# Moving stores to GpSimd's queue, fetching the first SwiGLU weights during w_out, interleaving two standard pairs by column group, and other pages for mid tiles

## The chip, the cores and the metric

The kernel runs on one core of a Trainium2 chip. The metric is the device time of one execution in microseconds (us). The kernel before took 1378.4 us, the median of three runs (1376.95 to 1379.79).

## The reference

One layer of a hybrid decoder on 1056 tokens (a prompt of 1024, and 8 sequences of 4 tokens with states of their own), D_MODEL 1024, all in float32. What matters here is the second half of the layer:

```python
merged = sigmoid(g_ssm) * br_ssm + sigmoid(g_pool) * br_pool
x  = x + gate1 * (merged @ w_out)                      # 1024 x 1024
h2 = rmsnorm(x, norm2_g) * (1 + scale2) + shift2
f_a, f_b = split(h2 @ w_ffn_in, 2)                     # 1024 x 2 * 2816
x  = x + gate2 * ((silu(f_a) * f_b) @ w_ffn_out)       # 2816 x 1024
y  = rmsnorm(x, normf_g)
```

Before it stand the modulation by the conditioning, the first norm, the input projection, a diagonal state-space mixer and a pooling mixer.

## The kernel before

All activations lie with features on the 128 partitions and the 1056 tokens along the free dimension, in eight tiles of 128 features. A product is made of three matmuls in a rounded format: each operand is split into a hi part (a cast) and a lo part (the rest), and hi x hi, hi x lo and lo x hi are summed (`feat`, L508). `split` (L487) makes the two parts of a weight tile: a cast on ScalarE (L491) and a subtraction on VectorE (L492). `load` (L482) fetches 512 KB of weights on SP into one of two `raw` buffers. The tokens are cut into three column groups, `GROUPS`: 0 to 384, 384 to 768, 768 to 1056.

The order of the instructions on TensorE and on SP's queue is that of the program. The order on VectorE, ScalarE and GpSimd is set by the build, by a schedule on a simulated time line. Work that is to run beside the matmuls is put among them by a `Pump` (L433): a generator that yields estimated microseconds; after each step of `feat` it is told how many have passed (`tick`, 3 x columns / 2400 a step), and it goes on when its time is due.

**w_out** (L1016 to L1031). Eight output tiles d for each column group g. w_out's first tile comes from the `wts` pool, the other seven lie split in the pool pE. After each product `residual` (L970) adds it to X[d], and `square` (L549) adds the squares to acc. In the last column group the finished X[d] is stored to DRAM (xr, L1028) on SP. After each column group its `norm2` is pumped: `rstd` (L578) sums acc over the partitions (L585), takes the reciprocal root on VectorE and spreads it by matmuls (L592) into R (L594); then for each of the eight tiles GpSimd multiplies x by R (L1002), ScalarE makes the hi part of h2 (L1003), VectorE the whole of it (`full`, L1008) and the lo part (L1012), and SP stores `full` to DRAM (hd, L1013). `full` has two buffers in pE for the first two groups; for the third it lies in acc's columns.

**ffn_in, standard pairs** (L1048, called at L1142). The hidden tiles k = 0 and 1 (NS = 2) of 22 are done in the ordinary way, one after the other, each with its three column groups: two products of eight steps (a and b), silu of a (L1059), times b (L1060), then `put_mid` (L1040) splits the result into mh and ml (L1043, L1044) and stores both to DRAM (md, L1046) on GpSimd's queue. The weights come through `ahead` (L499), which fetches and splits one tile ahead of the one in use. norm2 of the third group is still pumped during k = 0 and drained before its third group; `sums` follows on the pump.

**sums** (L1068). The pairs from k = 2 on use seven products in place of eight for a 2 x 2 block of features and tokens. `sums` builds the sums of h2's quarters that they need: for each of four tiles it fetches four quarters (bq, L1072) from hd on SP, makes four sums on VectorE (L1075 to L1078), and splits them into th and tl (L1085, L1086). bq, the sums and the tiles of put_mid share one ring of nine buffers in pool pF (`quart`, L1036). X's pages and acc's are reused by th and tl.

**Fast pairs** (L1154, called at L1196). `prep` (L1104) makes the seven weight operands of a pair, each with its hi part (L1109) and lo part (L1110), and `product` (L1127, matmuls L1133 to L1135) multiplies them. `ring` (L1098) says where each operand lies: three in pF with three buffers, four in `wts` with four. The operands of k = 2 are loaded and made after the standard pairs in the program.

**w_ffn_out** (L1216 to L1278). Three blocks of six hidden tiles, each for eight d, then a last stage of four hidden tiles (18 to 21) with the final norm. `fetch_mid` (L1208) brings mh and ml of one hidden tile back from DRAM on GpSimd's queue, into pages of the pool pP (26 pages, shared with X) or into the six buffers of `gpage` in pool pG (L1227). The tiles of the next block are asked for after d = 1 of each block (L1250).

Of the kernel before, what the change touches and what calls it, by code (L numbers as in the profile page):

```python
# [11 lines left out]
F32R = mybir.dt.float32r  # L12
# [443 lines left out]
def trunk(ctx: ExitStack, tc: tile.TileContext, A, O):  # L456
    nc = tc.nc
# [41 lines left out]
    def ahead(srcs):  # L499

        nxt = split2(srcs[0])
        for i in range(len(srcs)):
            cur, nxt = nxt, split2(srcs[i + 1]) if i + 1 < len(srcs) else None
            yield cur
# [3 lines left out]
    def feat(ps, w, x, g, kts, first=True, last=True):  # L508

        a, b = cols(g)  # L510
        for kt in kts:
            (wh, wl), (xh, xl) = w(kt), x(kt)
            pe.matmul(ps, wh, xh[:, a:b], start=first and kt == kts[0], stop=False)  # L513
            pe.matmul(ps, wh, xl[:, a:b], start=False, stop=False)  # L514
            pe.matmul(ps, wl, xh[:, a:b], start=False, stop=last and kt == kts[-1])  # L515
            tick(3 * (b - a) / 2400)

    def mmg(g):
        a, b = cols(g)
        return mm((128, b - a))  # L520
# [76 lines left out]
    def modulate_samples(xs, am, sm, k, t):  # L597

        bc = lambda m: m[:, k, None, 1:9].to_broadcast([128, 4, 8])
        f = lambda z: z.rearrange("p (s b) -> p s b", b=8)  # L600
        v.tensor_mul(f(t), f(xs), bc(am))
        v.tensor_add(f(t), f(t), bc(sm))
# [389 lines left out]
    def norm2(g):  # L992
        a, b = GROUPS[g]
        e = min(b, ST)
        yield 3.0
        for us in rstd(acc, g, R, 5.0):
            yield us if isinstance(us, float) else 1.0
        for k in range(8):
            t, (hi, lo) = tmp("xn"), h2x(k)
            sc, sh = mod[4][:, k, 0:1], mod[3][:, k, 0:1]  # L1000
            n = e - a
            gp.tensor_mul(t[:, 0:b - a], X[k][:, a:b], R[:, a:b])  # L1002
            act.activation(hi[:, a:e], t[:, 0:n], AF.Identity, bias=sh, scale=sc)  # L1003
            if g < 2:
                full = pE.tile([128, 384], F32, name="full", tag="full", bufs=2)
            else:
                full = acc[:, GROUPS[(g - k) % (g + 1)][0]:][:, 0:b - a]
            v.tensor_scalar(full[:, 0:n], t[:, 0:n], sc, sh, op0=MUL, op1=ADD)  # L1008
            if b > ST:
                modulate_samples(t[:, n:n + 32], mod[4], mod[3], k, full[:, n:])  # L1010
                act.copy(hi[:, e:b], full[:, n:])
            v.tensor_sub(lo[:, a:b], full[:, 0:b - a], fp(hi[:, a:b]))  # L1012
            nc.sync.dma_start(hd[k, :, a:b], full[:, 0:b - a])  # L1013
            yield 1.0

    with pool("pE") as pE:  # L1016
        wo = [next(wgen)]
        for d in range(1, 8):
            raw = load(A["w_out"][d])
            wo.append([split(raw[:, i], pE, "wo", 14) for i in range(2)])  # L1020
        for g in range(3):
            for d in range(8):
                ps = mmg(g)
                feat(ps, w8(wo[d]), mx, g, range(8))
                residual(d, g, ps, mod[2])
                square(X[d], g, acc, d == 0)
                if g == 2:
                    nc.sync.dma_start(xr[d], X[d])  # L1028
            pumps.append(Pump(norm2(g)))
        while len(pumps) > 1:  # L1030
            pumps.pop(0).drain()  # L1031
# [2 lines left out]
    third = ExitStack()  # L1034
    pF = third.enter_context(pool("pF"))
    quart = lambda n, dt=F32: pF.tile([128, 528], dt, name=n, tag="Q", bufs=9)  # L1036
    NS = 2
    wgen = ahead([A[n][k] for k in range(NS) for n in ("w_ffn_a", "w_ffn_b")])

    def put_mid(m, k, cut, eng=None):  # L1040

# [3 lines left out]
        for i, z in enumerate((hi, lo)):  # L1045
            gp.dma_start(md[k][:, i, cut], z)  # L1046

    def ffn_in(k, wa, wb):  # L1048
        for g in range(3):
            a, b = GROUPS[g]  # L1050
            n = b - a
            pa, pb = mmg(g), mmg(g)
            if k == 0 and g == 2:
                pumps.pop(0).drain()
                pumps.append(Pump(sums()))
            feat(pa, w8(wa), h2x, g, range(8))
            feat(pb, w8(wb), h2x, g, range(8))
            t = tmp("sa")
            act.activation(t[:, 0:n], pa, AF.Silu)  # L1059
            v.tensor_mul(t[:, 0:n], t[:, 0:n], pb)  # L1060
            put_mid(t[:, 0:n], k, slice(a, b))

# [3 lines left out]
    def sums():  # L1068
        for k in range(4):
            q = [quart("bq") for _ in range(4)]  # L1070
            for i, z in enumerate(q):
                nc.sync.dma_start(z, hd[k + 4 * (i // 2), :, 528 * (i % 2):528 * (i % 2) + 528])  # L1072
            b11, b12, b21, b22 = q
            f = {j: quart("bf") for j in (5, 3, 4, 6)}
            v.tensor_sub(f[4], b12, b22)  # L1075
            v.tensor_sub(f[5], f[4], b11)
            v.tensor_sub(f[3], b11, b12)
            v.tensor_add(f[6], f[5], b21)  # L1078
            for js in ((5, 3), (4, 6)):
                new = (lambda n: page(n, F32R)) if js[0] == 5 or k < 1 else (  # L1080
                    lambda n: pF.tile([128, NTOK], F32R, name=n, tag="T", bufs=6))
                hi, lo = new("th"), new("tl")
                for i, j in enumerate(js):
                    h, l = (z[:, 528 * i:528 * i + 528] for z in (hi, lo))
                    act.copy(h, f[j])  # L1085
                    v.tensor_sub(l, f[j], fp(h))  # L1086
                    TB[k, j] = (h, l)
            yield 6.0
# [8 lines left out]

    def ring(n, i):  # L1098
        t = "whi" if n == "whi" else "wlo"
        if i in (0, 3, 5):  # L1100
            return pF.tile([128, 512], F32R, name=n, tag="r" + t, bufs=3)
        return wts.tile([128, 512], F32R, name=n, tag=t, bufs=4)

    def prep(a11, a12, a21, a22):  # L1104
# [34 lines left out]
        ra, rb = load(A["w_ffn_a"][k]), load(A["w_ffn_b"][k])  # L1139
        return prep(ra[:, 0], ra[:, 1], rb[:, 0], rb[:, 1])  # L1140

    for k in range(NS):  # L1142
        wa = next(wgen)
        ffn_in(k, wa, next(wgen))
    for p in pumps:
        p.drain()
    pumps.clear()
# [87 lines left out]
    for bi, ks in enumerate(blocks):  # L1235
        for d in range(8):
            w, i = nxt, 8 * bi + d + 1
            nxt = o6(i) if i < 24 else None
            if bi == 2 and d >= 4:
                o4(d - 4)  # L1240
            pss = [mmg(g) for g in G3]
            for j, k in enumerate(ks):
                wd = lambda kt: tuple(z[:, 128 * (j % 3):128 * (j % 3) + 128] for z in w[j // 3])
                for g in range(3):
                    feat(pss[g], wd, lambda kt: mids[k], G3[g], [0], j == 0, j == 5)
            for g in range(3):
                residual(d, G3[g], pss[g], mod[5])
            if d == 1:
                for k in ((6, 7, 8, 9, 10, 11), (12, 13, 14, 15, 16, 17), (18, 19, 20, 21))[bi]:
                    fetch_mid(k, gpage if k in (9, 10, 11, 15, 16, 17, 20, 21) else mpage)  # L1250

    LAST = ((0, CUT[0]), CUT, (CUT[1], NTOK))
    acc3, R3 = page("acc3"), page("R3")
# [98 lines left out]
```

## Time and profile before

| | before |
|---|---|
| median of three runs | 1378.4 us (1376.95 to 1379.79) |
| the profiled execution | 1382.86 us, its span 1380.4 us |
| TensorE busy | 1318.2 us, 95% of the span |
| VectorE busy | 791.7 us, 57% |
| ScalarE busy | 440.3 us, 32% |
| GpSimd busy | 192.6 us, 14% |
| granted clock of TensorE, mean | 0.973 of 2.4 GHz |

The profile is of one execution; its times count from the span's start. Engines are named PE (TensorE, matmuls), PEld (its weight loads, which overlap the matmuls), DVE (VectorE), ACT (ScalarE), POOL (GpSimd) and SP; SPq and POOLq are the queues on which SP and GpSimd issue transfers. L1013 is line 1013 of the kernel. A matmul's duration runs to its modelled end and overlaps the next one, so the pace is read from starts.

### The profile page before, as it was taken

To read this page: it belongs to the slowest core of one execution; us is meant where nothing else is said; L and a number is where in the kernel's file an instruction comes from. 1 tells how busy PE (TensorE), PEld (TensorE's weight loads), DVE (VectorE), ACT (ScalarE), POOL (GpSimd) and SP (SyncE) were. 2 spreads that over 40 slices of the span, in tenths; PEclk is the share of its full clock that TensorE was granted. 3 is DMA by queue.
4 is the path that set the end of the run, shared out by engine and by line. 5 is a ranking of instruction groups with operands and counts; after the bars stand their busy time and mean duration, and the time that the engine had idled before them with its cause. 6 is when DMAs were issued, how large, how long until landed. Compare 5 with 4: busy or idle time off the path is not lost.

```text
span 1380.4 us, 23211 instructions
## 1 busy us (share of the span) xinstructions
PE 1318.2 (95%) x9248; PEld 1260.9 (91%) x9248; DVE 791.7 (57%) x1765; ACT 440.3 (32%) x840; POOL 192.6 (14%) x315
## 2 busy tenths in 40 slices
PE   5889999999999999979899999999999999999996
PEld 2789899999988899978899999999999999999985
DVE  8876895942115555665866666666666433333346
ACT  5423342234622332223433333333333211111124
POOL 3211222021000000222101001101101321000004
PEclk8899999999999999998999999999999999999998
DMA  9242213043535532153533333323323895232303
GB/s 382 85 132 62 77 52 91 23 113 118 180 128 170 185 131 77 47 202 119 166 108 109 105 98 109 110 93 109 121 82 109 308 350 174 75 116 78 94 24 126
DMA packets 75259, 173.95 MB, mean 126 GB/s; under 512 B 9808, under 2 KB 29456, under 8 KB 75152
## 3 DMA queue, kind: packets, MB, share of 16 engines
q1 hardware_dynamic: 47424, 105.77, 23.2%
q0 software_dynamic: 25280, 63.86, 14.1%
q10 hardware_dynamic: 2448, 2.84, 0.6%
q8 instruction: 72, 1.18, 0.4%
q14 instruction: 35, 0.29, 0.1%
HBM read 130.17 MB, written 42.27 MB: 125 GB/s over the span
## 4 chain that ended last, share of the span: by engine, by line
PE 38%; issue 10%; DVE 2%; DMA 2%; POOL 0%; DVEq 0%; ACT 0%; SPq 0%; POOLq 0%; ACTq 0%
PE b L1135 10%; PE b L1133 10%; PE b L1134 10%; PE mm L514 3%; PE mm L515 3%; PE mm L513 3%; DMA bq<-hd 1%; DMA ml<-md 1%; DMA mh<-md 0%; DVE tl L1086 0%; PE aux L592 0%; DVE xf L1264 0%; DVE bf L1075 0%; POOL mh L1211 0%; DVE sa L1060 0%
## 5 line engine op out<-in xcount | busy, mean ns | idle before, releaser
L513 PE MATMUL mm<-hh,whi 128*128 128x384 f32 (+1 forms) x864 | 290.4, 336 | 15.3 <-ACT whi L491 8.9
L514 PE MATMUL mm<-hl,whi 128*128 128x384 f32 (+1 forms) x864 | 284.7, 330 | 8.5 <-DVE hl L654 5.5
L515 PE MATMUL mm<-hh,wlo 128*128 128x384 f32 (+1 forms) x864 | 282.8, 327 | 0.0
L513 PEld LDWEIGHTS mm<-hh,whi 128*128 128x128 f32 x864 | 165.8, 192 | 30.2 <-issue 10.9
L1135 PE MATMUL b<-th,wlo 128*128 128x264 f32 x640 | 182.0, 284 | 1.1 <-DVE wlo L1110 1.1
L1133 PE MATMUL b<-th,whi 128*128 128x264 f32 x640 | 182.3, 285 | 0.0
L1134 PE MATMUL b<-tl,whi 128*128 128x264 f32 x640 | 181.9, 284 | 0.0
L492 DVE TENSOR_TENSOR wlo<-raw,whi 128x512 fp32r<-128x512 f32 (+1 forms) x144 | 92.0, 659 | 147.7 <-ACT whi L491 147.4
L514 PEld LDWEIGHTS mm<-hl,whi 128*128 128x128 f32 x864 | 166.0, 192 | 10.7 <-DVE hl L654 6.9
L514 PE MATMUL mm<-ml,whi 128*128 128x352 f32 (+3 forms) x528 | 171.7, 325 | 3.6 <-DMA ml<-md 3.6
L513 PE MATMUL mm<-mh,whi 128*128 128x352 f32 (+3 forms) x528 | 172.3, 326 | 2.2 <-DMA mh<-md 2.2
L515 PE MATMUL mm<-mh,wlo 128*128 128x352 f32 (+3 forms) x528 | 171.4, 325 | 0.0
L515 PEld LDWEIGHTS mm<-hh,wlo 128*128 128x128 f32 x864 | 165.9, 192 | 0.2 <-DVE wlo L492 0.2
L491 ACT CAST whi<-raw 128x512 fp32r<-128x512 f32 (+1 forms) x144 | 81.5, 587 | 245.9 <-PE mm L514 195.3
L1133 PE MATMUL b<-hh,whi 128*128 128x264 f32 x480 | 137.6, 287 | 2.8 <-ACT whi L1109 2.8
L1135 PE MATMUL b<-hh,wlo 128*128 128x264 f32 x480 | 137.6, 287 | 1.2 <-DVE wlo L1110 1.2
L1134 PE MATMUL b<-hl,whi 128*128 128x264 f32 x480 | 137.6, 287 | 0.0
L1135 PEld LDWEIGHTS b<-th,wlo 128*128 128x128 f32 x640 | 120.4, 188 | 1.3 <-DVE wlo L1110 1.3
L1134 PEld LDWEIGHTS b<-tl,whi 128*128 128x128 f32 x640 | 120.6, 188 | 0.0
L1133 PEld LDWEIGHTS b<-th,whi 128*128 128x128 f32 x640 | 120.3, 188 | 0.0
L1109 ACT CAST whi<-s 128x512 fp32r<-128x512 f32 x80 | 49.9, 623 | 179.5 <-PE b L1134 116.7
L514 PEld LDWEIGHTS mm<-ml,whi 128*128 128x128 f32 x528 | 100.2, 190 | 5.5 <-DMA ml<-md 4.8
(342 smaller groups left out, 2286.3 us busy)
## 6 DMA issues: line engine op xcount, KB each, us to landing
raw<-in_w_ada SPq DMA_DIRECT2D x64, 256.0 KB, 3.0
raw<-in_w_in SPq DMA_DIRECT2D x24, 512.0 KB, 4.1
mh<-md POOLq DMA_DIRECT2D x22, 528.0 KB, 7.5
ml<-md POOLq DMA_DIRECT2D x22, 528.0 KB, 8.3
raw<-in_w_ffn_a SPq DMA_DIRECT2D x22, 512.0 KB, 3.5
raw<-in_w_ffn_b SPq DMA_DIRECT2D x22, 512.0 KB, 3.6
md<-mh POOLq DMA_DIRECT2D x40, 264.0 KB, 2.3
md<-ml POOLq DMA_DIRECT2D x40, 264.0 KB, 2.6
```

What stands on the lines that cost most here:

```text
L491: act.copy(hi, raw)
L492: v.tensor_sub(lo, raw, fp(hi))
L513: pe.matmul(ps, wh, xh[:, a:b], start=first and kt == kts[0], stop=False)
L514: pe.matmul(ps, wh, xl[:, a:b], start=False, stop=False)
L515: pe.matmul(ps, wl, xh[:, a:b], start=False, stop=last and kt == kts[-1])
L1109: act.copy(hi, x)
L1133: pe.matmul(o, wh, xh, start=first and k == 0, stop=False, skip_group_check=True)
L1134: pe.matmul(o, wh, xl, start=False, stop=False, skip_group_check=True)
L1135: pe.matmul(o, wl, xh, start=False, stop=k == 3, skip_group_check=True)
```

## The change

The stores of h2 (hd) and of x (xr) leave SP's queue: `norm2` collects them and issues them on GpSimd after every second tile, x's stores in the third group beside h2's. `full` of the third group lies in the ring `quart` and no longer in acc. The weights of k = 0 are fetched and split ahead of w_out's third column group, those of k = 1 right after w_out, into a ring of four buffers in pF. The standard pairs run in the order (k, g) = (0,0), (0,1), (1,0), (1,1), (0,2), (1,2), with norm2 of the third group drained before (1,1) and `sums` pumped from there. In `ring` the products 3, 4 and 5 take pF's buffers (four each) in place of 0, 3 and 5 (three each). The mid tiles 15, 16, 17 and 21 go to pages of pP and no longer to pG; 18 and 19 go to pG and no longer to pP.

```diff
--- before.py
+++ after.py
@@ -992,6 +992,7 @@
     def norm2(g):
         a, b = GROUPS[g]
         e = min(b, ST)
+        stores = []
         yield 3.0
         for us in rstd(acc, g, R, 5.0):
             yield us if isinstance(us, float) else 1.0
@@ -1004,13 +1005,19 @@
             if g < 2:
                 full = pE.tile([128, 384], F32, name="full", tag="full", bufs=2)
             else:
-                full = acc[:, GROUPS[(g - k) % (g + 1)][0]:][:, 0:b - a]
+                full = quart("full")
             v.tensor_scalar(full[:, 0:n], t[:, 0:n], sc, sh, op0=MUL, op1=ADD)
             if b > ST:
-                modulate_samples(t[:, n:n + 32], mod[4], mod[3], k, full[:, n:])
-                act.copy(hi[:, e:b], full[:, n:])
+                modulate_samples(t[:, n:n + 32], mod[4], mod[3], k, full[:, n:n + 32])
+                act.copy(hi[:, e:b], full[:, n:n + 32])
             v.tensor_sub(lo[:, a:b], full[:, 0:b - a], fp(hi[:, a:b]))
-            nc.sync.dma_start(hd[k, :, a:b], full[:, 0:b - a])
+            stores.append((hd[k, :, a:b], full[:, 0:b - a]))
+            if g == 2:
+                stores.append((xr[k], X[k]))
+            if k % 2:
+                for s in stores:
+                    gp.dma_start(*s)
+                stores.clear()
             yield 1.0
 
     with pool("pE") as pE:
@@ -1019,13 +1026,13 @@
             raw = load(A["w_out"][d])
             wo.append([split(raw[:, i], pE, "wo", 14) for i in range(2)])
         for g in range(3):
+            if g == 2:
+                fw = [split2(A[n][0]) for n in ("w_ffn_a", "w_ffn_b")]
             for d in range(8):
                 ps = mmg(g)
                 feat(ps, w8(wo[d]), mx, g, range(8))
                 residual(d, g, ps, mod[2])
                 square(X[d], g, acc, d == 0)
-                if g == 2:
-                    nc.sync.dma_start(xr[d], X[d])
             pumps.append(Pump(norm2(g)))
         while len(pumps) > 1:
             pumps.pop(0).drain()
@@ -1034,8 +1041,10 @@
     third = ExitStack()
     pF = third.enter_context(pool("pF"))
     quart = lambda n, dt=F32: pF.tile([128, 528], dt, name=n, tag="Q", bufs=9)
+    for n in ("w_ffn_a", "w_ffn_b"):
+        raw = load(A[n][1])
+        fw.append([split(raw[:, i], pF, "r", 4) for i in range(2)])
     NS = 2
-    wgen = ahead([A[n][k] for k in range(NS) for n in ("w_ffn_a", "w_ffn_b")])
 
     def put_mid(m, k, cut, eng=None):
 
@@ -1045,20 +1054,16 @@
         for i, z in enumerate((hi, lo)):
             gp.dma_start(md[k][:, i, cut], z)
 
-    def ffn_in(k, wa, wb):
-        for g in range(3):
-            a, b = GROUPS[g]
-            n = b - a
-            pa, pb = mmg(g), mmg(g)
-            if k == 0 and g == 2:
-                pumps.pop(0).drain()
-                pumps.append(Pump(sums()))
-            feat(pa, w8(wa), h2x, g, range(8))
-            feat(pb, w8(wb), h2x, g, range(8))
-            t = tmp("sa")
-            act.activation(t[:, 0:n], pa, AF.Silu)
-            v.tensor_mul(t[:, 0:n], t[:, 0:n], pb)
-            put_mid(t[:, 0:n], k, slice(a, b))
+    def ffn_in(k, g):
+        a, b = GROUPS[g]
+        n = b - a
+        pa, pb = mmg(g), mmg(g)
+        feat(pa, w8(fw[2 * k]), h2x, g, range(8))
+        feat(pb, w8(fw[2 * k + 1]), h2x, g, range(8))
+        t = tmp("sa")
+        act.activation(t[:, 0:n], pa, AF.Silu)
+        v.tensor_mul(t[:, 0:n], t[:, 0:n], pb)
+        put_mid(t[:, 0:n], k, slice(a, b))
 
 
 
@@ -1097,8 +1102,8 @@
 
     def ring(n, i):
         t = "whi" if n == "whi" else "wlo"
-        if i in (0, 3, 5):
-            return pF.tile([128, 512], F32R, name=n, tag="r" + t, bufs=3)
+        if i in (3, 4, 5):
+            return pF.tile([128, 512], F32R, name=n, tag="r" + t[1:], bufs=4)
         return wts.tile([128, 512], F32R, name=n, tag=t, bufs=4)
 
     def prep(a11, a12, a21, a22):
@@ -1139,9 +1144,11 @@
         ra, rb = load(A["w_ffn_a"][k]), load(A["w_ffn_b"][k])
         return prep(ra[:, 0], ra[:, 1], rb[:, 0], rb[:, 1])
 
-    for k in range(NS):
-        wa = next(wgen)
-        ffn_in(k, wa, next(wgen))
+    for k, g in ((0, 0), (0, 1), (1, 0), (1, 1), (0, 2), (1, 2)):
+        if (k, g) == (1, 1):
+            pumps.pop(0).drain()
+            pumps.append(Pump(sums()))
+        ffn_in(k, g)
     for p in pumps:
         p.drain()
     pumps.clear()
@@ -1247,7 +1254,7 @@
                 residual(d, G3[g], pss[g], mod[5])
             if d == 1:
                 for k in ((6, 7, 8, 9, 10, 11), (12, 13, 14, 15, 16, 17), (18, 19, 20, 21))[bi]:
-                    fetch_mid(k, gpage if k in (9, 10, 11, 15, 16, 17, 20, 21) else mpage)
+                    fetch_mid(k, gpage if k in (9, 10, 11, 18, 19, 20) else mpage)
 
     LAST = ((0, CUT[0]), CUT, (CUT[1], NTOK))
     acc3, R3 = page("acc3"), page("R3")
```

## Rows read from the trace of the kernel before

**Rows 1.** Windows: stretch, its length, busy us of PE, PEld, DVE, ACT, POOL; clock, DMA, GB/s.

```profile
600.00:612.00 12.00, 12.00 (x91) 11.79 (x89) 11.88 (x26) 5.27 (x9) 6.00 (x5) 1.00 0.50 194
612.00:620.00 8.00, 0.02 (x1) 0.00 (x0) 2.84 (x10) 0.89 (x2) 0.00 (x0) 0.78 0.96 347
621.00:627.00 6.00, 6.00 (x19) 5.77 (x20) 2.46 (x4) 1.57 (x3) 0.00 (x0) 0.53 0.25 88
647.00:654.00 7.00, 6.33 (x25) 5.98 (x26) 3.31 (x9) 1.93 (x6) 1.13 (x2) 0.51 0.88 277
1313.00:1319.60 6.60, 5.33 (x13) 4.41 (x14) 0.68 (x1) 0.58 (x1) 0.00 (x0) 0.50 0.07 26
```

**Rows 2.** TensorE's waits, whole span: us in total, times, longest.

```profile
PE mm L513 <- ACT whi L491: 10.1, 2, 8.9
...
PE mm L514 <- DMA ml<-md: 3.6, 4, 1.7
...
PE mm L514 <- DVE hl L1012: 3.0, 3, 1.4
PE b L1133 <- ACT whi L1109: 2.8, 1, 2.8
...
PE mm L513 <- DMA mh<-md: 2.2, 2, 1.9
```

**Rows 3.** Timeline of TensorE, 611 to 682: start, us, engine, line, operation, idle before.

```profile
611.73 0.29 PE L515 MATMUL mm<-hh,wlo 128*128 128x288 f32 x1
...
620.96 0.69 PE L513 MATMUL mm<-hh,whi 128*128 128x384 f32 x1 [8.94 <-ACT whi L491]
...
655.35 0.34 PE L513 MATMUL mm<-hh,whi 128*128 128x384 f32 x1
...
678.41 0.29 PE L515 MATMUL mm<-hh,wlo 128*128 128x288 f32 x1
681.47 0.59 PE L1133 MATMUL b<-hh,whi 128*128 128x264 f32 x1 [2.76 <-ACT whi L1109]
```

**Rows 4.** Timeline of SP's queue, 500 to 720, merged.

```profile
612.25 3.08 SPq L1028 DMA_DIRECT2D xr<-xr  x3
615.43 0.41 SPq L484 DMA_DIRECT2D raw<-in_w_ffn_a  x1
...
648.72 1.94 SPq L1072 DMA_DIRECT2D bq<-hd  x4
...
658.11 16.76 SPq L1072 DMA_DIRECT2D bq<-hd  x12
674.92 0.49 SPq L484 DMA_DIRECT2D raw<-in_w_ffn_a  x1
```

**Rows 5.** Timeline of all engines, 615 to 657.

```profile
615.56 0.46 DVE L557 TENSOR_TENSOR acc<-acc,sq 128x288 f32<-128x288 f32 x1 [0.57 <-ACT sq L556]
...
634.14 0.40 ACT L594 COPY R<-aux 128x288 f32<-128x288 f32 x1 [0.20 <-PE aux L592]
...
656.01 0.71 DVE L1075 TENSOR_TENSOR bf<-bq 128x528 f32<-128x528 f32 x1
```

**Rows 6.** Groups: the casts (page), then those of 634 to 650 by form; busy, mean ns.

```profile
L492 DVE TENSOR_TENSOR wlo<-raw,whi 128x512 fp32r<-128x512 f32 (+1 forms) x144 | 92.0, 659 | 147.7 <-ACT whi L491 147.4
...
L1002 POOL TENSOR_TENSOR xn<-xr,R 128x288 f32<-128x288 f32 x8 | 7.0, 880 | 3.5 <-DVE acc L601 1.9 <-DVE acc L602 1.6
...
L1046 POOL DMA_DIRECT2D md<-mh x2 | 1.2, 600 | 25.9 <-ACT mh L1043 25.9
```

**Rows 7.** DMA issues, 500 to 720: count, KB each, median us to landing.

```profile
hd<-full SPq DMA_DIRECT2D x16, 192.0 KB, 1.8
...
xr<-in_x POOLq DMA_DIRECT2D x2, 528.0 KB, 5.6
md<-mh POOLq DMA_DIRECT2D x4, 192.0 KB, 2.4
```

**Rows 8.** Timeline of GpSimd, 1250 to 1330: the last fetch.

```profile
1307.84 0.54 POOL L1211 DMA_DIRECT2D ml<-md  x1
```

## The prediction

> **What bounds the kernel now.** I read the windows of the stages first, then TensorE's waits, then the timelines of SP and of all engines, and last GpSimd's fetches before the final stage. TensorE works without a break almost everywhere, so a change pays only where it stands still or runs at the lower clock. Two places do both.
>
> The first lies between w_out and the fast pairs (the pairs from k=2 on, with seven products each). w_out's last matmul ends at 611.73 + 0.29 = 612.0, the first of ffn_in starts at 620.96, the first of the fast pairs at 681.47 [rows 3]. The second standard pair ran at the full 2.4 GHz from 655.35 to 678.7, 23.35 us. Two pairs and about 1 us of sums for the norm are 47.7 us of work, but 69.5 us pass, so 21.8 are lost. The terms: 8.9 us for the cast of the first weights (of the 10.1 in two waits) and 3.0 for h2's lo parts [rows 2]; 2.8 before the fast pairs, for a cast [rows 2]; and the clock, granted at 0.53 of full over 6 us after the first stop (the lower level, 1.2 GHz, for nearly all of it; 2.8 us lost) and at 0.51 over 7 us after the second (6.33 busy, so 3.1) [rows 1]. That makes 20.6.
>
> What stands behind the waits is SP's queue, which works strictly in the order of the program. The weights of k=0 are asked for at 615.43, right behind the last stores of x, which wait for the last residuals; those of k=2 at 674.92, behind all sixteen bq loads [rows 4]. GpSimd carries only multiplications there.
>
> The second place is the start of the third block of w_ffn_out and of the last stage: waits for mid tiles of 3.6 and 2.2 us [rows 2]. The last fetch is issued at 1307.84 [rows 8], because its buffer was read to the end by the block before; afterwards the clock is granted at 0.50 over 6.6 us, 5.33 of them busy [rows 1].
>
> **The change, part by part.**
>
> *Weights of k=0 ahead.* Their two loads stand on SP ahead of w_out's last column group, with nothing before them that waits for a residual, and a's casts need buffers free since the GLU. b's casts reuse those of w_out's d=0, free early in the group. So the 8.9 us and the 2.8 behind them go. The loads of k=1 follow on SP at once. Their four casts on VectorE, 0.66 us each [rows 6], fall near 612, since their buffers lie over w_out's, and are wanted only 17 us later, when (1,0) starts. What is late next is the sum of squares.
>
> *That sum.* The norm's first matmul stands in TensorE's order behind seven steps of 0.53 us (23.35 us hold 16 such steps for each 384 of 2 x 1056 columns), at 615.7. The sum's last add ran 615.56 to 616.02 [rows 5] with VectorE busy 11.88 of the last 12 us [rows 1]. It gets the casts besides (2.6 us), and norm2(1), with two `full` buffers and stores in pairs, can hold it for a store's landing (2.4 us). So TensorE stops for 0.3 to 5 us; I take **2**. From the first weight matmul to R, norm2(2)'s factor, were 13.2 us (620.96 to 634.14, [rows 3, 5]), 2.8 of them clock. R then stands at 612.0 + 10.4 + 2 = 624.4, 9.7 earlier.
>
> *Stores on GpSimd.* norm2(0) and (1) issue sixteen stores there, and norm2(2) eight of h2 and eight of x, sixteen more, in pairs of k. A store holds GpSimd for 0.6 us and a multiplication for 0.88 [rows 6]: 7.0 + 16 x 0.6 = 16.6 us for norm2(2), where SP's last store was issued some 14 us after R. Queued behind each pair are the multiplications of the next two k. The first sums need k=0 and 4, so six k, 12.5 us, and a landing: 1.8 us from SP, 2.4 for a tile of mid from GpSimd, 5.6 for a whole x tile loaded on GpSimd's queue [rows 7]. The x stores (0.54 MB each) lie between those of h2, so I take 4 from inside 2.4 to 5.6. The first bq load comes 16.5 us after R, against 14.6 (634.14 to 648.72, [rows 4, 5]): at 640.9. The 347 GB/s that stores and loads together moved from 612 to 620 [rows 1] say that 5.5 MB of stores need 16 us, about the same, so the queue is no second bound.
>
> *Sums to fast pairs.* From there to the first sum were 7.3 us (to 656.01, [rows 5]). b's weights of k=1 no longer share it, x's last stores do: 4 to 10, I keep 7.3. From the first sum to the fast pairs were 25.5, a chain of buffers, sums and the next loads, and at its end the weights of k=2 on the same queue. That order stays. It loses two casts of k=1's weights that lay in it (1.3 us): I take 24, within 20 to 26. The fast pairs start at 640.9 + 7.3 + 24 = **672.2, 9.3 earlier**. TensorE is free at 612.0 + 2 + 47.7 = 661.7, so of 20 us that the interleaving could give, about half is given back as a longer stop here; the stop after h2's lo parts (3.0 and 3.1) is gone, as (0,2) comes only after four blocks of 8.5 us. The clock falls at the fast pairs as it did, no change.
>
> *The ring of the seven products.* Products 0, 1, 2 and 6 take the buffers of k=0's weights, free before the last block; 3 to 5 take a fourth buffer each. Nothing at 0: TensorE's work covers it, and without that cover it costs one cast, 0.66.
>
> *Pages of mid.* 12 to 17 all go to pages that the first block frees, a whole block ahead; 18 to 20 to the buffers of 9 to 11, free after the second block, and 21 to a page of the second block. All are in long before their use. The waits of 3.6 + 2.2 and the clock's 5.33 x 0.5 = 2.7 go: **8.5**. Between 5.8, if the clock falls for another reason, and 8.5. The fetches are as many as before, only GpSimd's order differs.
>
> **Sum.** 9.3 + 8.5 = 17.8. The profiled execution took 1382.9 (span 1380.4), so 1365.1 by its own count. The median of the runs is 1378.4, 4.5 lower, which I lay to that one execution: **1360.6**.
>
> **Rivals.**
>
> *The chain of sums is hidden.* If bq loads follow one another faster (each waits only for buffers, and with less traffic on the same engines), the fast pairs start where TensorE is free, at 660 to 662, and the clock does not fall there. For it: TensorE's 661.7 is not far off. Against: three rounds of at least 6 us stand between. Gain 20 + 8.5, to 31 with the clock: about 1350. Chance 0.17.
>
> *GpSimd becomes the bound.* Stores wait there for VectorE's tiles, and the multiplications behind them wait too; norm2(2) then takes 22 to 26 us instead of 16.6, and the fast pairs start at 678 to 682. For it: the multiplications already waited 3.5 us for VectorE [rows 6]. The store at 0.60 us with VectorE busy for most of that stretch [rows 6] speaks against. Gain 0 to 4 and 8.5: about 1368. Chance 0.20.
>
> The page "SBUF — State Buffer" of the Trainium skill (section "Who interferes with whom") says that a VectorE instruction in a two-port mode keeps GpSimd from writing the descriptors of its DMAs. By that rule the stores would start late and this rival would be the case; the 0.60 us shows no such hold, though an issue time is not a landing.
>
> *Slower than before.* norm2(1) has two `full` buffers, and now a store in pairs from GpSimd. Three times a pair waits for the pair before it to land. At 2.4 us that costs some 5, and h2 of the second column group is ready at 617 to 618, before (0,1) wants it at 620.5. The whole gain of 17.8 is eaten when each such wait is 9 us or more (three of them 27, less the 3 of slack and the 5 counted), since TensorE then stops in (0,1) and norm2(2) queues behind. With 11 us each, TensorE would stop 6 us longer than that: 1384. Only the 5.6 of an x tile points that way. Chance 0.05.
>
> *The weights are not ahead.* If the casts for k=0 are put behind the residuals on VectorE and ScalarE, whose order the build's schedule sets, part of the 8.9 stays and the chain of sums with it: gain of 8.5 alone, 1370. Chance 0.04.
>
> **How the numbers follow.** The forecast, 1356 to 1366, has the remaining 0.54. The range joins to it most of the hidden chain and most of GpSimd's case, 1350.5 to 1370; left out are the slower case, the far ends of both and a little more. The runs before lie within 2.8 us, 0.2%, which is about what a measurement can tell from no change. Faster by more than that: 0.93; within it 0.02; slower 0.05.
>
> **What would show it.** Right: no idle time of TensorE between 612 and 615; a wait of 1 to 3 us for the sum of squares (L585); R near 624; the first bq load near 641; a stop before L1133 longer than the 2.8 of before, 8 to 12 us, ended by the cast of k=2's weights; no waits for mh and ml in the third block and in the last stage, and a granted clock of 1.00 there. Wrong: fast pairs at 662 (hidden chain), R to the first bq load over 20 us (GpSimd's bound), a wait for hl in (0,1) (the slower case), or an idle stretch at 612 ended by a cast. A wait for a page of mid 21 would break the second term.

## The result, and the profile after

The changed kernel took **1364.06 us**, median of four runs (1359.18 to 1366.05), beside 1379.1 for the kernel before (four runs, 1376.95 to 1382.0): ratio 0.9884, interval 0.985 to 0.9918, so 1.2% faster. The profiled execution took 1366.05 us with a span of 1363.2, 17.2 us under the span of before.

TensorE's waits over the whole span of the changed kernel (us in total, times, longest) answer to [rows 2]:

```profile
PE b L1138 <- ACT whi L1114: 11.4, 1, 11.4
...
PE aux L585 <- DVE acc L557: 6.7, 2, 3.7
...
PE b L1140 <- DVE wlo L1115: 1.7, 2, 1.2
...
PE mm L513 <- ACT whi L491: 1.4, 1, 1.4
```

The 8.9 before ffn_in, h2's lo parts and the waits for mh and ml are gone. The one before the first fast product grew from 2.8 to 11.4, and one for the sum of squares (L585) is new. Of L585's two, the 3.7 is the final norm's, which the kernel before has too; the other is the 3.01 in the timeline of TensorE, which answers to [rows 3]:

```profile
618.69 0.33 PE L585 MATMUL aux<-acc,ones 128*32 128x72 f32 x8 [3.01 <-DVE acc L557]
...
675.76 0.59 PE L1138 MATMUL b<-hh,whi 128*128 128x264 f32 x1 [11.36 <-ACT whi L1114]
...
1089.16 0.33 PE L513 MATMUL mm<-mh,whi 128*128 128x352 f32 x1
...
1298.00 0.37 PE L513 MATMUL mm<-mh,whi 128*128 128x448 f32 x1
```

The same places in the kernel before, its first fast product being at 681.47 [rows 3]:

```profile
1096.38 0.32 PE L513 MATMUL mm<-mh,whi 128*128 128x352 f32 x1
...
1308.48 0.37 PE L513 MATMUL mm<-mh,whi 128*128 128x448 f32 x1
```

These rows split the 17.2 us. The fast pairs start 5.7 earlier; w_ffn_out 7.2 earlier (1.5 more); w_ffn_out up to the last stage takes 208.84 in place of 212.10 (3.3); the last stage 65.20 in place of 71.92 (6.7). By these two executions 7.2 come from ahead of w_ffn_out and **10.0 from the pages of mid**. The profiled execution of before (1382.86) was slower than all four of its timed runs, and the runs below split the gain otherwise: 3 to 5 and 12.

Windows of the changed kernel (columns as in [rows 1]):

```profile
612.00:620.00 8.00, 4.99 (x34) 4.56 (x34) 6.42 (x16) 3.69 (x6) 4.19 (x6) 0.98 0.66 268
620.00:624.00 4.00, 4.00 (x16) 4.00 (x16) 2.65 (x11) 2.61 (x6) 1.09 (x2) 0.61 0.26 102
...
664.40:675.70 11.30, 0.01 (x1) 0.00 (x0) 7.83 (x13) 3.93 (x8) 1.07 (x2) 0.64 0.66 216
675.70:682.00 6.30, 5.05 (x24) 4.75 (x25) 6.30 (x12) 3.51 (x8) 1.07 (x2) 0.57 0.22 58
...
1227.00:1298.00 71.00, 71.00 (x442) 71.00 (x441) 26.52 (x63) 11.26 (x21) 2.12 (x4) 1.00 0.33 104
...
1302.50:1309.10 6.60, 6.60 (x34) 6.15 (x33) 3.30 (x5) 1.64 (x3) 0.00 (x0) 1.00 0.02 5
...
1298.00:1363.20 65.20, 51.51 (x337) 48.87 (x336) 41.69 (x106) 21.99 (x42) 16.77 (x16) 0.90 0.19 67
```

After the stop of 3.01 the clock is granted at 0.61 over 4 us of full work, about 1.6 us lost. Beyond 664.40 TensorE has nothing left to do until the fast pairs, which start at the lower level. In the third block of w_ffn_out (1227 to 1298) TensorE never stands still. Beside it and the last stage, the same views of the kernel before:

```profile
1237.50:1308.48 70.98, 68.50 (x423) 67.67 (x422) 24.24 (x57) 10.76 (x20) 2.12 (x4) 1.00 0.30 92
1308.48:1380.40 71.92, 55.12 (x337) 50.63 (x336) 41.59 (x106) 21.99 (x42) 16.74 (x16) 0.86 0.24 87
```

TensorE's idle time fell by 3.1 (16.80 to 13.69) and its busy time by 3.6 (55.12 to 51.51, the same 337 matmuls) in the last stage: about half idle time and half slower matmuls, most of that the clock.

Why the sum of squares is late is seen on GpSimd. Its timeline in the changed kernel (597 to 617), with norm2(1)'s factor on ScalarE, and a tile of h2 and the last add on VectorE:

```profile
595.70 0.48 ACT L594 COPY R<-aux 128x384 f32<-128x384 f32 x1 [2.29 <-PE aux L592]
...
597.22 0.53 POOL L1019 DMA_DIRECT2D xr<-xr  x1 [3.52 <-DVE xr L979]
597.77 1.99 POOL L1003 TENSOR_TENSOR xn<-xr,R 128x384 f32<-128x384 f32 x2
...
605.81 0.55 POOL L1019 DMA_DIRECT2D xr<-xr  x1 [2.52 <-issue]
...
614.40 1.04 POOL L1003 TENSOR_TENSOR xn<-xr,R 128x384 f32<-128x384 f32 x1
614.41 1.25 DVE L1009 TENSOR_SCALAR full<-xn,mod,mod 128x384 f32<-128x384 f32 x1
...
618.18 0.46 DVE L557 TENSOR_TENSOR acc<-acc,sq 128x288 f32<-128x288 f32 x1 [0.51 <-ACT sq L556]
```

The same in the kernel before, where norm2(1)'s factor stands at the same moment and the last add is the row of [rows 5], 615.56:

```profile
595.72 0.48 ACT L594 COPY R<-aux 128x384 f32<-128x384 f32 x1 [2.16 <-PE aux L592]
596.28 1.99 POOL L1002 TENSOR_TENSOR xn<-xr,R 128x384 f32<-128x384 f32 x2 [21.76 <-ACT R L594]
...
608.76 1.19 POOL L1002 TENSOR_TENSOR xn<-xr,R 128x384 f32<-128x384 f32 x1 [0.39 <-DVE acc L557]
```

The build put x's stores (L1019, xr) between norm2(1)'s multiplications, and all that is behind a store on GpSimd waits with it. Ahead of the first multiplication that is 3.52 us for a residual of w_out, which costs the multiplication 1.5. Ahead of the store at 605.81 it is 2.52 us, for which the profile shows no cause: the residual adds ahead of it had ended by 604.06. The last of the eight multiplications starts 18.7 us after the factor, not 13.0, and VectorE, which works on their results between its adds, starts the last add 22.5 after it, not 19.8. In the run below with x's stores back on SP and h2's still on GpSimd (e9_x_on_sp) the last multiplication starts 14.9 after, so most of the 5.7 is x's stores.

VectorE's own instructions last longer beside a multiplication: the tile at 614.41 takes 1.25 us, one with no multiplication beside it 0.48, and the add at 597.50, beside the first two multiplications, 2.58 against 0.46. Multiplications that come later thus also meet VectorE's last adds; what part of the delay that is, no run separates.

### The profile page after: what moved, and what is told of

The parts are those of the page before. It is cut to its first block, busy times and chain, and to the rows that moved or that the text cites. A ratio compares the mean times of both kernels' runs of the same rounds, so it can differ in the third digit from the quotient of the medians.

```text
span 1363.2 us, 23205 instructions
## 1 busy us (share of the span) xinstructions
PE 1305.5 (96%) x9248; PEld 1252.1 (92%) x9248; DVE 791.4 (58%) x1765; ACT 440.5 (32%) x840; POOL 207.6 (15%) x347
## 4 chain that ended last, share of the span: by engine, by line
PE 82%; DVE 8%; DMA 4%; issue 4%; ACT 1%; POOL 1%; SPq 0%; POOLq 0%; DVEq 0%; ACTq 0%
PE mm L513 17%; PE mm L514 16%; PE mm L515 16%; PE b L1139 10%; PE b L1138 10%; PE b L1140 10%; PE aux L611 2%; DMA bq<-hd 1%; PE yp L381 1%; PE vp L320 1%; POOL xf L1273 1%; DMA x<-in_x 1%; PE yp L377 1%; DVE wlo L492 1%; DVE full L1009 1%
## 5 line engine op out<-in xcount | busy, mean ns | idle before, releaser
L1138 PE MATMUL b<-hh,whi 128*128 128x264 f32 x480 | 137.2, 286 | 11.8 <-ACT whi L1114 11.4
L1138 PEld LDWEIGHTS b<-hh,whi 128*128 128x128 f32 x480 | 91.3, 190 | 12.2 <-ACT whi L1114 11.6
L513 PEld LDWEIGHTS mm<-mh,whi 128*128 128x128 f32 x528 | 99.3, 188 | 0.8 <-issue 0.2
```

The lines of the kernel that those rows point to most:

```text
L1138: pe.matmul(o, wh, xh, start=first and k == 0, stop=False, skip_group_check=True)
```

## The experiments

Twelve runs followed: ten new versions, and the changed kernel and one version a second time. The table has their times with the ratio to the kernel before on the same chip, and stages of the profiled execution. Executions differ by some 4 us before norm2(1) (its factor stands between 592.6 and 597.1), so the stages count from the copy of norm2(1)'s factor ("R1": 595.72 before, 595.70 after); "sq" is the last add of the squares, "R2" norm2(2)'s factor, "bq" its first load, "sum" the first sum, "fast" the first fast product.

| run | us, median (range) | ratio, interval | sq | R1 to R2 | R2 to bq | bq to sum | sum to fast | R1 to fast |
|---|---|---|---|---|---|---|---|---|
| before | 1379.1 (1376.95 to 1382.0) | | 19.8 | 38.4 | 14.6 | 7.3 | 25.5 | 85.8 |
| after | 1364.06 (1359.18 to 1366.05) | 0.9884 (0.985 to 0.9918) | 22.5 | 31.2 | 13.0 | 11.1 | 24.7 | 80.1 |
| e1_old_pages | 1376.02 (1374.04 to 1378.76) | 0.9974 (0.9958 to 0.9991) | 22.4 | 31.2 | 13.0 | 11.2 | 24.7 | 80.0 |
| e8_pages_only | 1367.83 (1367.23 to 1370.41) | 0.9917 (0.9897 to 0.9938) | 19.8 | 37.0 | 14.6 | 7.1 | 24.6 | 83.3 |
| e2_not_interleaved | 1364.36 (1362.22 to 1365.70) | 0.9885 (0.9862 to 0.9908) | 22.5 | 29.6 | 9.7 | 8.7 | 28.1 | 76.2 |
| e3_early_k2 | 1362.07 (1361.73 to 1364.82) | 0.9873 (0.9854 to 0.9892) | 22.5 | 31.2 | 13.0 | 11.8 | 12.5 | 68.5 |
| e4_stores_on_sp | 1359.49 (1358.33 to 1362.67) | 0.9854 (0.9833 to 0.9875) | 19.9 | 29.1 | 15.4 | 7.3 | 26.6 | 78.4 |
| e9_x_on_sp | 1369.57 (1368.0 to 1370.84) | 0.9926 (0.9906 to 0.9946) | 25.7 | 34.4 | 13.0 | 11.3 | 25.0 | 83.7 |
| e5_sp_early | 1360.04 (1358.39 to 1360.44) | 0.9855 (0.9836 to 0.9874) | 19.9 | 28.5 | 15.4 | 6.6 | 14.4 | 64.9 |
| e7_sp_early_reorder | 1362.44 (1360.47 to 1364.06) | 0.9879 (0.9856 to 0.9901) | 19.9 | 28.5 | 15.4 | 7.4 | 13.7 | 64.9 |
| e12_after_again | 1363.39 (1361.78 to 1366.71) | 0.9882 (0.9859 to 0.9905) | 22.5 | 32.2 | 13.0 | 11.3 | 25.3 | 81.9 |
| e10_no_pairs | 1362.07 (1361.89 to 1363.57) | 0.9873 (0.9852 to 0.9893) | 22.5 | 32.4 | 13.0 | 11.0 | 25.3 | 81.6 |
| e11_sp_no_interleave | 1361.02 (1356.97 to 1363.36) | 0.9859 (0.9837 to 0.9881) | 19.8 | 29.1 | 15.4 | 6.2 | 25.4 | 76.1 |
| e13_stores_on_sp_again | 1360.37 (1358.63 to 1360.83) | 0.9856 (0.9835 to 0.9876) | 19.8 | 28.8 | 15.4 | 7.3 | 25.5 | 77.1 |

The stages of before and of the run with new pages alone are the same code up to the fast pairs and differ by 2.5 us; a single profile is read no closer than that.

**The old pages, in the changed kernel** (e1_old_pages).

```diff
-                    fetch_mid(k, gpage if k in (9, 10, 11, 18, 19, 20) else mpage)
+                    fetch_mid(k, gpage if k in (9, 10, 11, 15, 16, 17, 20, 21) else mpage)
```

> The changed kernel with the old pages for the mid tiles 15 to 21, all else kept. Theory of two separate terms (the pages give 8.5 us by the prediction, 10.0 by the two profiles: 3.3 in the third block, 6.7 in the last stage): 1372 to 1375 against 1364, with the waits for mh and ml back at about 5.7 us and everything up to the second block as in the changed kernel. Rival (the waits were a matter of where the blocks fell against other transfers, and go with the earlier start): 1364 to 1366, no waits for mid tiles.

12.0 us slower than the changed kernel, just above the range of the first theory, and only 3.2 faster than the kernel before beside it: that is all the rest of the change is worth here. TensorE's waits for mid are back:

```profile
PE mm L514 <- DMA ml<-md: 3.2, 4, 1.6
PE mm L513 <- DMA mh<-md: 2.1, 2, 1.7
```

**The new pages alone, in the kernel before** (e8_pages_only; the same line the other way round).

> The kernel before with the new pages for the mid tiles alone. Theory of two separate terms: 11 to 12 us below the kernel before, 1367 to 1369, as much as the old pages cost the changed kernel; no waits for mh and ml from the third block on, everything up to the fast pairs as before. By the prediction's term it would be 8.5 us, 1370 to 1371. Rival (the pages help only together with the rest): within 3 us of the kernel before.

11.8 us faster than before, with the 8.67 us wait ahead of ffn_in still there. Taken away and added alone, the pages are worth the same 12 us: four fifths of the change's 15.0 by medians.

**The pairs one after the other** (e2_not_interleaved).

```diff
-    for k, g in ((0, 0), (0, 1), (1, 0), (1, 1), (0, 2), (1, 2)):
-        if (k, g) == (1, 1):
+    for k, g in ((0, 0), (0, 1), (0, 2), (1, 0), (1, 1), (1, 2)):
+        if (k, g) == (0, 2):
```

> The changed kernel with the standard pairs one after the other, (0,0) (0,1) (0,2) (1,0) (1,1) (1,2), the norm drained and the sums pumped from (0,2). Theory A (the chain norm, stores, sums, loads of k=2 on SP sets the start of the fast pairs, TensorE has 11 us of slack before it): the idle time moves to a wait for h2 of the third group at (0,2), the fast pairs start within 3 us of 675.8, total within 3 us of 1364. Theory B (the order of TensorE's own work gave the gain): the fast pairs start 6 us or more later, total 1370 or more.

The same time. TensorE now waits for h2 in (0,2), six times, 2.4 us in all, and starts the fast pairs without a wait, but stops three times among their first products (1.25 to 1.61 us each). The interleaving moves idle time from one place to the other.

**The weights of k = 2 ahead of the bq loads** (e3_early_k2).

```diff
+    w2 = [load(A[n][NS]) for n in ("w_ffn_a", "w_ffn_b")]
...
-        ra, rb = load(A["w_ffn_a"][k]), load(A["w_ffn_b"][k])
+        ra, rb = w2 if k == NS else (load(A["w_ffn_a"][k]), load(A["w_ffn_b"][k]))
```

> The changed kernel with the two loads of k=2 put on SP ahead of the loads of the sums. Theory A1 (k=2's weights wait only because they stand behind sixteen bq loads): the first matmul of the fast pairs comes where TensorE is free, at 664 to 666 in place of 675.8, TensorE then stops before the second product, for the last sums, until about 674; total 3 to 5 us less, 1359 to 1361. Theory A2 (the sums are the whole chain, the loads come in time with them): fast pairs no earlier than 673, total 1363 to 1365.

The wait of 11.4 is gone and the fast pairs start 11.6 us earlier after R1, as theory A1 has it, but the time falls by 2 only, inside the intervals and between the two forecasts. The timeline of TensorE in that run:

```profile
672.72 0.59 PE L1139 MATMUL b<-th,whi 128*128 128x264 f32 x1 [6.50 <-ACT whi L1115]
676.95 0.59 PE L1139 MATMUL b<-th,whi 128*128 128x264 f32 x1 [1.59 <-ACT th L1091]
679.37 0.59 PE L1140 MATMUL b<-tl,whi 128*128 128x264 f32 x1 [1.83 <-DVE tl L1092]
```

The second product stops for an operand whose parts are made behind the sums, and the next for the sums themselves (th, tl). The last weights on SP's queue and the chain of sums end within a few us of each other, so undoing one shows the other.

**The stores back on SP, one per tile** (e4_stores_on_sp).

```diff
-            stores.append((hd[k, :, a:b], full[:, 0:b - a]))
...
+            nc.sync.dma_start(hd[k, :, a:b], full[:, 0:b - a])
...
+                if g == 2:
+                    nc.sync.dma_start(xr[d], X[d])
```

> The changed kernel with the stores of h2 and x back on SP, each right behind its tile, all else kept. Theory A (the gain of the first stage comes from the weights fetched ahead, and the stores in pairs only lengthen the norm): the wait for the sum of squares falls from 3.0 to under 1.5 us, R stands at 623 to 625 in place of 626.9, the fast pairs start 2 to 4 us earlier, total 1360 to 1362. Theory C (the stores have to leave SP, or they hold the weights of k=1): TensorE waits for a cast at (1,0), total 1367 or more.

Faster than the changed kernel, half a us below theory A's range. The stop for the sum of squares is 0.39, R2 comes 2.1 earlier after R1, and although the first bq load then takes 2.4 longer, the first sum follows it 3.9 sooner.

**x's stores alone back on SP, h2's left on GpSimd in pairs** (e9_x_on_sp).

```diff
-            if g == 2:
-                stores.append((xr[k], X[k]))
...
+                if g == 2:
+                    nc.sync.dma_start(xr[d], X[d])
```

> The changed kernel with the stores of x alone back on SP, right behind each residual; those of h2 stay on GpSimd in pairs. Theory P (the pairs hold the norm, since full has two buffers): the wait for the sum of squares stays at about 3 us, total 1363 to 1365. Theory X (x's stores, which the build put on GpSimd between its multiplications from 590 to 617, hold the norm): the wait falls under 1.5 us, total 1360 to 1362, as with both kinds of store on SP.

Neither theory held: it is 5.5 above the changed kernel's median. VectorE, TensorE and GpSimd in its timeline:

```profile
614.28 1.13 POOL L1017 DMA_DIRECT2D hd<-full  x2 [3.34 <-DVE xr L979]
...
620.38 0.48 DVE L1009 TENSOR_SCALAR full<-xn,mod,mod 128x384 f32<-128x384 f32 x1 [5.98 <-DMA hd<-full]
...
621.28 0.47 PE L585 MATMUL aux<-acc,ones 128*32 128x72 f32 x8 [6.25 <-DVE acc L557]
```

Without x's stores between them the multiplications run ahead, and now the two `full` buffers bind: a pair of stores is issued at 614.28, beside the last of x's stores and the loads of k = 1's weights on SP (issued to 614.29, and at 614.38 and 614.86), and VectorE stands 5.98 us for a landing, the last add of the squares behind it. Which of SP's transfers made the landing long wasn't tried. The median landing of h2's tiles in this stretch (596 to 625) was 3.5 us; in the changed kernel, in the same view:

```profile
hd<-full POOLq DMA_DIRECT2D x8, 192.0 KB, 2.2
```

**Stores on SP and early weights of k = 2 together** (e5_sp_early; both edits above).

> The changed kernel with both kinds of store on SP and the loads of k=2 ahead of those of the sums. Theory S (with the loads early, the sums' chain is the bound: first product at TensorE's leisure, then a stop before the second): gains of the two edits add, 2 us below the run with the stores on SP, 1357 to 1359; a stop of 5 to 9 us before the second product. Rival (loads and sums are the same wait, so the second edit brings nothing): 1359 to 1361.

No gain over the stores on SP alone (the rival's time, with theory S's stop), although the fast pairs start 13.5 us earlier after R1: the second product stops 6.18 us, the next ones 1.56 and 1.83. As long as the sums end where they do, an early start of the pairs is given back.

**The same with the third product of the first fast pair ahead of the second** (e7_sp_early_reorder).

```diff
-        step(b2, 1, 5, True)
...
+        if k == NS:
+            product(b1, cur[2], 1, False)
+            step(b2, 1, 5, True)
```

> As the run with stores on SP and early loads, and in the first fast pair the product that needs no sums (the third) is done before the second one. Theory S: TensorE has 2.9 us more work before it stops for the sums, and the stop is shorter by as much: 2 to 3 us below that run, 1354 to 1356. Rival (the stop is set by the weight operands, which VectorE makes in the order of the products behind the sums, and the third operand comes after the second): no gain, within 1 us of that run.

Slower by 2.4 than the run before it, by medians, which neither theory forecast: one stop of 11.82 us ahead of the moved product takes the place of three.

```profile
672.78 0.59 PE L1135 MATMUL b<-hh,whi 128*128 128x264 f32 x1 [11.82 <-ACT p L1173]
```

The product adds to the first product's result, so it waits for ScalarE's copy of that result (p, L1173), which the build put behind casts of the sums:

```profile
671.60 0.63 ACT L1087 CAST th<-bf 128x528 fp32r<-128x528 f32 x1
672.14 0.59 ACT L1173 COPY p<-b 128x528 f32<-128x528 f32 x1
```

As built, the moved product thus waited for the sums as well, and the run cannot tell whether work that does not would shorten the stop.

**The changed kernel again** (e12_after_again), beside the three that follow.

> The changed kernel once more, beside the three that follow, so that differences of 2 to 5 us among them are read on one chip with the same runs of the kernel before. Expected by every theory: 1362 to 1366 us, ratio 0.987 to 0.990, a stop of about 3 us of TensorE for the sum of squares (L585).

1363.39, and the stop of 2.99. Over both sets the changed kernel has nine runs with a median of 1363.39, the version with stores on SP eight with a median of 1360.3 (the mean of the middle two, 1359.97 and 1360.58).

**Stores on GpSimd, but one at a time** (e10_no_pairs).

```diff
-            if k % 2:
+            if True:
```

> Stores stay on GpSimd's queue, but each is issued in its own step instead of in pairs of two. Theory P (pairing is the price: norm2(1) has two buffers for h2's tiles, a pair of stores holds both, and VectorE's next tile, and behind it the sum of squares, waits for a landing): the stop for the sum of squares falls from 3.0 to under 1 us, R comes 3 to 4 us earlier against w_out's start, 1359 to 1361 us, like the kernel with the stores on SyncE. Theory Q (the queue itself is the price: a store on GpSimd waits behind multiplications there and holds up those behind it): the stop stays at 2 to 4 us, 1363 to 1366 us.

The stop stays at 3.00 and every stage as it was: not the pairing but the queue makes it (theory Q), though the time, 1.3 below the changed kernel beside it, lies between the two forecasts.

**Early weights and new pages, without the interleaving and without GpSimd's stores** (e11_sp_no_interleave; two edits above together).

> The first weights fetched ahead and the new pages alone: stores as before on SyncE, one per tile, and the pairs one after the other as before. Against the run with the new pages alone (1367.8) it shows what the early weights are worth, against the run with stores on SyncE and interleaved pairs (1359.5) what the interleaving is worth when the sum of squares is not late. Theory A (the chain of sums sets the start of the fast pairs, so the interleaving only moves idle time): 1358 to 1361, the early weights worth 7 to 10, fast pairs within 2 us of those of the interleaved kernel. Theory B (with R earlier, the interleaving does hide the third column group's late h2): 1362 to 1365, with a stop of 3 us or more in the third column group and a lower clock after it that is not made good.

6.8 us below the pages alone, so that is what the early weights are worth (with the new ring and the new place of `full`, which no run takes apart), and 0.7 above the interleaved version beside it, within the intervals. Theory A by the interleaving's price and the fast pairs, with the early weights just under its 7 to 10: TensorE stops for h2's lo parts, 1.77 and 1.39, and 2.69 before the fast pairs, which start 76.1 after R1, against 77.1.

**The stores on SP again** (e13_stores_on_sp_again).

> The version with the stores back on SyncE once more, on the same chip as the changed kernel. If moving the stores to GpSimd cost 3 to 5 us, as the first run says: 1358.5 to 1361, and 3 to 5 us below the changed kernel's own time here. If the first run's lead was chance (the stages before w_out differ by up to 3 us from one execution to another): within 2 us of the changed kernel.

1360.37, 3.0 below the changed kernel beside it. Its rows for the sum of squares:

```profile
613.98 0.46 DVE L557 TENSOR_TENSOR acc<-acc,sq 128x288 f32<-128x288 f32 x1 [0.57 <-ACT sq L556]
...
614.49 0.33 PE L585 MATMUL aux<-acc,ones 128*32 128x72 f32 x8 [0.37 <-DVE acc L557]
```

Step by step, by medians: pages -11.8 (1379.66, the kernel before beside that run, to 1367.83), early weights -6.8 (to 1361.02), interleaving -0.7 (to 1360.37), stores on GpSimd +3.0 (to 1363.39); the versions of the last two steps were run side by side, the others not. The steps add up to 16.3, the change by its own comparison to 15.0. The changed kernel without its move of the stores beats both kernels.

## Why the prediction was right, and where two errors met

The total was right: 1360.6 forecast, 1364.06 measured, inside the forecast's own range of 1356 to 1366; by the profiled executions' spans 17.8 forecast, 17.2 measured. But the terms were 9.3 and 8.5. By the two profiles they measured 5.7 to 7.2 and 10.0, by runs 3.2 to 4.6 (the old pages in the changed kernel against before; the changed kernel against the new pages alone, by ratios) and 12. The interval of the first of these, 1.2 to 5.8 us, leaves out the 9.3. So one term was about 5 too large, the other about 3.5 too small, and that they nearly cancel is luck. Part of the first error was in the execution that the prediction was read from: up to w_ffn_out it took 2.4 us longer after R1 than the same code did in the run with the new pages alone (500.7 against 498.3).

*Weights ahead.* Right: TensorE passes from w_out to ffn_in without a stop, the 8.9 is gone, and the edit is worth 6.8 to 8.0 by runs (8.0 is the difference of the ratios, 0.0058 of 1380). The 6.8 to 8.0 is this edit by itself; the move of the stores takes 3.0 of it back. The casts of k = 1 did not get in the way of the sum: their VectorE halves ran from 626.07.

*The sum of squares.* "I take 2" measured 3.01, within 0.3 to 5, but for another reason than the two given. Without the stores on GpSimd the stop is 0.37 with the casts there all the same. What was missed is where the build puts x's stores: the prediction laid them between h2's in norm2(2), as the program has them; they need only the residuals, and the schedule moved them among norm2(1)'s multiplications. The lower clock after the stop, 1.6 us, was not in the sum at all. So R2 stood at 626.91, not 624.4. (The 0.53 us a step is 23.35 over 44 steps, eight for each 384 of 2 x 1056 columns, not sixteen; the figure is right.)

*Stores on GpSimd.* "The first bq load comes 16.5 us after R" measured 13.0, since x's stores were no longer there, and the "7.3" from bq to the first sum measured 11.1: the first loads then wait for h2's stores, the last of which left GpSimd at 645.25. The two sum to 24.1 against 23.8: the error was in the place, not in the sum. The forecast costed this edit at about 2 us after R2, beside a share of the 2 at the sum; by runs it cost 3.0, most of it at the sum of squares.

*Sums to fast pairs.* 24 forecast, 24.7 measured. So the fast pairs started at 675.76, not 672.2: 2.5 late from R2, 0.35 from R2 to the first sum, 0.7 after it. That the long stop is ended by the cast of k = 2's weights, 8 to 12 us, was right (11.36), and so was that idle time only moves there. That the interleaving is then worth nothing by itself (0.3 us by medians with the stores on GpSimd, 0.7 with them on SP, both within the intervals) follows, and the prediction did not draw it. A further 1.5 us came between the fast pairs and w_ffn_out. The runs that enter them after one long stop took 412.5 to 413.5 us there, the ones that stop in several places 413.7 to 415.0; why wasn't tried.

*Pages of mid.* The 5.8 of waits was right (TensorE's idle time fell by 2.5 in the third block and 3.1 in the last stage). So was the clock's 2.7 in its stretch. In the kernel before, thirteen matmuls took from 1313.74 to 1319.63, 5.36 us without the stop of 0.53; at the pace of the rows behind them, 0.204, they take 2.65:

```profile
1313.74 0.74 PE L513 MATMUL mm<-mh,whi 128*128 128x448 f32 x1 [1.90 <-DMA mh<-md]
1315.01 0.74 PE L514 MATMUL mm<-ml,whi 128*128 128x448 f32 x1 [0.53 <-DMA ml<-md]
...
1319.63 0.37 PE L514 MATMUL mm<-ml,whi 128*128 128x448 f32 x1
...
1321.87 0.36 PE L513 MATMUL mm<-mh,whi 128*128 128x448 f32 x1
```

What the sum lacked is busy time beside the stops that is no work either: a matmul ahead of a stop runs out (0.32 us where the next start would come after 0.16), and the one behind it is slow to hand on. That fits the 0.8 us of the third block, which has three stops, and 0.5 in the last stage ahead of 1313.74; the other 0.4 of its 3.6 was not followed. By runs the edit is worth 12; why 2 more than by the profiles isn't shown.

*The rivals.* A hidden chain of sums (1350): no, and the runs with k = 2's weights early stop all the same, for weight parts that are made behind the sums and for the sums themselves. GpSimd as the bound: in a small way and in another norm, norm2(1), not through late stores of norm2(2); the last multiplication there started 18.7 us after the factor. The rule on VectorE's two-port mode (the Trainium skill, page "SBUF — State Buffer", section "Who interferes with whom") has no part here that a row shows: the sixteen stores from 588 to 626 were issued in 0.53 to 0.60 us each, with VectorE busy 10.13 of 12 us from 600. The one wait ahead of a store that the profile leaves open, the 2.52 us up to 605.81, went on while VectorE stood idle (605.05 to 605.66), so the rule does not cover it all; what made it stays open. The slower rival, norm2(1)'s two buffers, is real: it decides with x's stores on SP and h2's on GpSimd (5.98 us), which is the half-way version and not the change; one such wait there cost 5.5, short of the 17.8 to be eaten.

## What to carry to other kernels

A gain before a chain that ends elsewhere is given back at that chain; measure each part of such a change alone and by taking it away, for a right total can hide a part that costs. A transfer put on the queue of a computing engine makes that engine wait for the transfer's data, and where the build orders the engine, the transfer need not stay where the program has it: look for who is queued behind the earliest place at which it could be issued.

## What was not expected of the hardware

The clock answered stops of the same size in different ways. In the kernel before, a stop of 1.66 us in the third block left it at 1.00. Its timeline row, and the window behind it (columns as in [rows 1]):

```profile
1246.20 0.43 PE L514 MATMUL mm<-ml,whi 128*128 128x352 f32 x1 [1.66 <-DMA ml<-md]
```

```profile
1245.00:1252.00 7.00, 5.80 (x36) 5.80 (x37) 2.20 (x6) 0.52 (x2) 0.00 (x0) 1.00 0.20 58
```

With the old pages in the changed kernel a stop of 1.58 at the same place was followed by the lower level (0.50 from 1238.5 to 1240, 1.00 again from 1242). Each stood behind two shorter stops, of 0.54 and 0.27 us before and of 0.23 and 0.33 here. The same two views of that run:

```profile
1238.59 0.66 PE L514 MATMUL mm<-ml,whi 128*128 128x352 f32 x1 [1.58 <-DMA ml<-md]
```

```profile
1236.00:1245.00 9.00, 7.08 (x34) 6.59 (x33) 2.38 (x6) 0.51 (x1) 0.00 (x0) 0.81 0.27 91
```

So what the clock adds to a wait can't be read from the wait's length alone; for the pages of mid, by the profiles, 2.7 of the 10.0 went to the lower clock, all of it in the last stage.
